# Low parts of the mixers' projection weights: an accumulating DMA in place of a subtraction on GpSimd or VectorE

## The chip, the cores and the metric

One NeuronCore of a Trainium2 chip runs one transformer layer. The metric is device time in microseconds (us) of one execution; the kernel before took 799.82 us, the median of three runs (797.5 to 801.35). Engine names in the views: PE is TensorE's matmul, PEld its weight load, DVE is VectorE, ACT is ScalarE, POOL is GpSimd, SP is the engine that issues most loads.

## The reference, cut to what matters

512 tokens of 1024 features go through one decoder layer. Only its first half is touched by the change:

```python
u = rms_norm(x, g_mix) @ w_in              # 3072 columns: q, k, v of two mixers
ya = diff_attention(qa, ka, va, lam, ...)  # 4 heads, softmax of two score maps
yb = stick_breaking_attention(qs, ks, vs)  # 8 heads, sigmoids and a running product
h = x + concat(ya, yb) @ w_out
h = h + cross_attention(...)               # then the MLP and a last norm
```

All of it is float32. The kernel keeps that precision with three float32r products for each product of matrices.

## The kernel before, in words

**Two parts of a float32.** Each matrix is held as hi + lo, both float32r. `split` (L107) makes them: ScalarE copies the source into hi with rounding (L109), then one engine subtracts, lo = source - hi (L113). `mm3` (L101) issues three products: lines L102, L103 and L104 are hi by hi, hi by lo, lo by hi, in the order of left and right operand. In a projection whose weights are on the right, as for the values (v), it is L103 that reads the weights' lo.

**Pieces of weights.** Weights come in pieces of 128 partitions by 1024 numbers, 512 KB, in the order of the list `stream`. A piece is loaded by SP into a tile `raw` (L122), and `parts` (L125) splits it into tiles `hi` and `lo`. There are three buffers each of raw, hi and lo, so the load of piece n+3 waits until lo of piece n has been made, and hi of piece n+3 waits until TensorE has done with piece n. `take` (L138) hands out a piece and has the next one or two made. The list `lo_eng` says who does the subtraction: VectorE at first, GpSimd from the start of the mixers (L717) up to unit 4, VectorE again from there (L731).

**The mixers.** Units u = 0 to 3 are heads of differential attention, u = 4 to 7 pairs of stick-breaking heads. A unit has four steps (query blocks). In a step TensorE makes scores `sc` (L378 to L382), ScalarE exponentials (L394) or sigmoids (L404, L405), VectorE the weights `e` (L391 to L399, or L407 and L409), and TensorE transposes them (L422) one half-step later. Between the steps `fill` runs projection work of later units on TensorE: how much is in the table `FILL`, which the change leaves alone. The scores have one buffer, so the scores of a step wait until ScalarE has read those of the step before. The projections of the fill are, in this order: keys k1, values va0 (two pieces, a and b), keys k2, k3, values va1 (a, b), then q4, k4, vb0 (a, b), q5, k5, q6, k6, q7, k7, vb1 (a, b); w_out follows (its first piece is called o0 here). Queries and keys of the first mixer go through `rope` (L290), in which VectorE multiplies, GpSimd multiplies (`sh`, L295) and VectorE adds (`rt`, L296); ScalarE and VectorE then write the two parts of q or k.

**What sets the order.** TensorE's order is that of the code. In the mixers ScalarE, VectorE and GpSimd are put in order by the scheduler when the kernel is built; each engine then runs its list strictly in that order.

Of the kernel before, what the change touches and what calls it, by code (L numbers as in the profile page):

```python
# [14 lines left out]
AF = mybir.ActivationFunctionType  # L15
ALU = mybir.AluOpType
# [6 lines left out]
NEG = -1e30  # L23
# pairs of feature tiles of a quarter in the order in which the up projection makes them
DOWN = (0, 2, 1, 3)
EPS = 1e-6
# PE microseconds of filler work after each half of a step, per unit
FILL = (
# [10 lines left out]
TWO_PI = 6.2831853071795864769252867665590057683943  # L39
# ROPE_THETA ** (-arange(0, 16, 2) / 16) in float32  # L40
FREQ = [1.0, 0.1939227432012558, 0.03760603070259094, 0.007292664609849453,
# [4 lines left out]
def two_pi_parts(bits, n):  # L46
    """2 pi as a sum of n floats of the given number of bits each."""
    from decimal import Decimal, getcontext

    getcontext().prec = 60  # L50
    rest = Decimal("6.28318530717958647692528676655900576839433879875021164194988918")
    parts = []
    for _ in range(n):
        e = math.frexp(float(rest))[1]
        unit = Decimal(2) ** (e - bits)
        q = (rest / unit).to_integral_value(rounding="ROUND_DOWN") * unit
        parts.append(float(q))
        rest -= q
    return parts
# [3 lines left out]
def tile_decoder_layer(  # L63
# [34 lines left out]

    # Every matrix product is the sum of three products of parts: a float32 is the
    # exact sum of two float32r, a = hi + lo, and lo * lo lies below float32's last place.  # L100
    def mm3(o, l, r, first, last):  # L101
# [4 lines left out]
    def split(hi, lo, src, scale=1.0, eng=None):  # L106
        """hi + lo = src * scale; scale is a number or a column of one per partition."""  # L107
        if isinstance(scale, float):
            nc.scalar.activation(hi, src, AF.Copy, bias=0.0, scale=scale)  # L109
        else:  # L110
            nc.scalar.activation(hi, src, AF.Identity, bias=0.0, scale=scale)
        if isinstance(scale, float) and scale == 1.0:
            (eng or nc.vector).tensor_tensor(lo, src, hi.bitcast(F32), ALU.subtract)  # L113
        else:
            nc.vector.scalar_tensor_tensor(lo, src, scale, hi.bitcast(F32), ALU.mult, ALU.subtract)

    # Pieces of weights in the order of their use; each is loaded and split some pieces ahead.
    stream, loaded, taken, lo_eng = [], [], [0], [nc.vector]
# [6 lines left out]
    def parts(raw, dst=None):  # L125
        if dst is None:
            dst = [wp.tile(raw.shape, F32R, tag=n, name=n) for n in ("hi", "lo")]
        split(dst[0], dst[1], raw, eng=lo_eng[0])
        return dst
# [13 lines left out]
    def proj_n(act, o, n, last=8, ahead=2):  # L143
        """o = (act @ w)^T for the next 128 columns of weights and an activation with features
        first; what the steps cost on TensorE."""
        whi, wlo = take(ahead)
# [10 lines left out]
    def rsqrt(pool, v, n, name, eng=None):  # L157
        """v ** -0.5 for a few columns: a guess from the exponent and three Newton steps."""
        y = pool.tile([P, n], F32, tag=name, name=name)
# [74 lines left out]

# [1 line left out]
    ident = cp.tile([P, P], F32, name="ident")  # L236
# [8 lines left out]
    for i in range(2):  # L245
        m = cp.tile([P, P], BF16, name=f"mask{i}")
        nc.gpsimd.memset(m, 0.0)
        # kept where q - k - i >= 0
        nc.gpsimd.affine_select(m, m, pattern=[[-1, P]], compare_op=ALU.is_ge, fill=NEG,
# [7 lines left out]
    R = cp.tile([P, 8, S], F32, name="resid")  # L257
# [1 line left out]
    att = ExitStack()  # L259
# [7 lines left out]

    # A query tile holds two heads of 64 features: q[h] has the two parts of head h below each other,
    # hi in its own rows; k[h] has hi of head h in both halves, k[2] lo of both heads in their rows.
    def q_tiles():  # L270
# [70 lines left out]

    # Work that fills TensorE between the steps of the mixers, in its order.
    class Filler:
# [20 lines left out]
    class Mixer:  # L364
        """One step of a mixer: a head of differential attention, or a pair of stick-breaking heads."""

# [4 lines left out]
        def scores(self, i):  # L371
            """Scores of query block i against the keys up to its end, for both halves of the rows."""
            q, k = self.qk
# [37 lines left out]
        def transpose(self, i):  # L411
            """Weights of query block i into blocks i, i + 3, ... (one for each key block)."""
            if not self.w:
# [66 lines left out]
    def by_key(w, j):  # L480
        """Weights of key block j, and the columns of query tokens they go to."""
        b0 = 11 if j == 3 else 4 * j
# [61 lines left out]

    # x with features first waits in DRAM for the residual
    x_ps = {}
# [25 lines left out]

    # TensorE runs at its full clock only after some microseconds of work
    wps = mm_tile()
# [41 lines left out]
    fill = Filler()  # L616
    # angles, and their remainders by 2 pi in three steps, each exact
    freq = sp.tile([P, 8], F32, name="freq")
# [15 lines left out]
    nc.gpsimd.tensor_scalar(ang, ang, math.pi - 2e-7, -(math.pi - 2e-7), ALU.min, ALU.max)  # L634
    # cos(a) = sin(pi / 2 - |a|)
    anc = sp.tile([P, 4, 8], F32, name="anc")
# [7 lines left out]
    nc.scalar.activation(cs, anc, AF.Sin, bias=0.0, scale=1.0)  # L644
    # the queries and keys of the first mixer are an eighth; put_k makes the keys whole again
    rsx = rs8.unsqueeze(2)
# [26 lines left out]
    put_k(ks[0], rope(ps), 8.0)  # L673
    # lambda
    lp = sp.tile([P, 2, 64], F32, name="lp")
# [12 lines left out]

# [1 line left out]
    def add_qk(u):  # L690
# [25 lines left out]
    add_v(vb, 1, vb_tile, vb_proj)  # L716
    lo_eng[0] = nc.gpsimd  # L717
    fill.run(9.1)

    prev = None  # L720
    for u in range(8):
# [7 lines left out]
        fill.unit = u  # L729
        if u == 4:  # L730
            lo_eng[0] = nc.vector  # L731
# [32 lines left out]

# [1 line left out]
    bp = ctx.enter_context(tc.tile_pool(name="bp", bufs=1, reuse_waits="tile"))  # L766
# [58 lines left out]

# [1 line left out]
    kx = [xp.tile([P, 8, M], F32R, name=f"kx{i}") for i in range(2)]  # L827
    vx = [xp.tile([P, 2, D], F32R, name=f"vx{i}") for i in range(2)]
    for n in range(8):
# [3 lines left out]
        if n == 1:  # L833
            # scale of the queries, folded into the softmax
            tr = tr_tile().rearrange("p (t n) -> p t n", t=4)
# [109 lines left out]

# [1 line left out]
    # The up projection is done in 2 x 2 blocks (of features, of inputs, of tokens) with Winograd's seven  # L947
    # products for eight: for W = A11 .. A22 (feature block, input block) and activations B11 .. B22
    # (input block, token block)
    #   S1 = A21 + A22, S2 = S1 - A11, S3 = A11 - A21, S4 = A12 - S2  # L950
    #   T1 = B12 - B11, T2 = B22 - T1, T3 = B22 - B12, T4 = T2 - B21
    #   U2 = A11 B11 + S2 T2, U3 = U2 + S3 T3
    #   C11 = A11 B11 + A12 B21, C12 = U2 + S1 T1 + S4 B22, C21 = U3 - A22 T4, C22 = U3 + S1 T1
    ml = ctx.enter_context(tc.tile_pool(name="ml", bufs=1, reuse_waits="tile"))
# [52 lines left out]
    def weave(a, b):  # L1007
        """Steps of two lists in turn."""
        return [x for pair in itertools.zip_longest(a, b) for x in pair if x is not None]

    # the steps of the MLP: products of the up projection beside pieces of the down projection
    def up_steps(u):
# [141 lines left out]
    def up_norm():  # L1154
        for t in range(4):
            junk = wp.tile([P, D], F32, tag="raw", name="junkh")
            nc.scalar.activation(junk, acc[:, t, :], AF.Square, bias=0.0, scale=1.0, accum_out=ss[:, t:t + 1])
        # relu(r u)^2 = r^2 relu(u)^2 for r > 0: the square of the scale goes onto the down products
        nc.gpsimd.tensor_scalar(ss, ss, 1.0 / D, EPS, ALU.mult, ALU.add)
# [23 lines left out]
    upper_half = slice(512, D)  # L1183
    # the sum of squares of a token and acc * g_final over the columns done
    fs = ml.tile([P, 4, 3], F32, name="fs")
# [13 lines left out]
    for t in range(4):  # L1199
        squares_of(t, 0, slice(0, 512))  # L1200
        gained(t, slice(0, 512))
    # h = -0.5 (mean + eps), the part of it that is done
    nc.vector.tensor_scalar(fc, fs[:, :, 0], -0.5 / D, -0.5 * EPS, ALU.mult, ALU.add)
# [17 lines left out]
    def root(h):  # L1221
        # (-2 h) ** -0.5: a guess from the exponent and three Newton steps
        r = ml.tile([P, 1], F32, tag="fr", bufs=2, name="fr")
# [8 lines left out]
    def finish(t, cols, r):  # L1232
        """cols: the columns that are still to be multiplied by g_final."""
        tok = slice(t * P, (t + 1) * P)
# [54 lines left out]
```

## Time and profile before

| | |
|---|---|
| median of 3 runs | 799.82 us (797.5 to 801.35) |
| span of the profiled execution | 795.6 us |
| PE busy | 769.2 us, 97% of the span |
| DVE, ACT, POOL busy | 553.1, 423.9, 104.7 us |
| the mixers with what is left of the q and k of unit 0 | about 40 to 250 us of the span |

The span runs from the first to the last instruction of one profiled execution, and the median of the timed runs lies 4.2 us above it; the profiled execution has no time of its own beside its span. TensorE is busy nearly all the time, so what can be won or lost is in the few stretches in which it stands still, and in the stretches in which its clock is granted at half.

### The profile page before, as it was taken

Reading aid. Unit: us, or ns where it says so; the run is one execution under the profiler, and the core shown is the slowest. Engines: PE = TensorE matmul, PEld = TensorE weight load, DVE = VectorE, ACT = ScalarE, POOL = GpSimd, SP = SyncE. Lnnn points to the kernel's source line nnn. Section 1 sums busy time; section 2 is a strip of 40 time slices with the busy share of each in tenths; the row PEclk is TensorE's granted clock in tenths of the full one; section 3 lists DMA queues with packets and bytes.
Section 4 is the critical chain, followed back from the end, with each engine's and each line's share of the span. In section 5 each row is a group of like instructions: output and inputs, shape, how many; then the busy total and the mean of one; then the engine's idle time right before and its main releaser. Section 6 shows DMA issues by size and latency. Waiting matters only on the chain.

```text
span 795.6 us, 11669 instructions
## 1 busy us (share of the span) xinstructions
PE 769.2 (97%) x4552; PEld 668.1 (84%) x4552; DVE 553.1 (70%) x829; ACT 423.9 (53%) x723; POOL 104.7 (13%) x200
## 2 busy tenths in 40 slices
PE   7997999999979999999999999999999999999996
PEld 6886788877867899888888899888988899889885
DVE  3889877689896874445746989556865486647745
ACT  5646655777756554254535788333543454345622
POOL 7166443420050011000000030000000000000000
PEclk9998999999989999999999999999999999999998
DMA  9522111211113446224361044332334233230402
GB/s 267 164 81 79 54 54 54 75 35 56 50 53 118 148 130 188 82 77 133 102 191 53 27 162 131 106 107 79 114 99 127 86 92 121 80 105 1 133 1 106
DMA packets 83977, 77.98 MB, mean 98 GB/s; under 512 B 2545, under 2 KB 70290, under 8 KB 83922
## 3 DMA queue, kind: packets, MB, share of 16 engines
q1 hardware_dynamic: 83120, 76.16, 30.8%
q0 software_dynamic: 160, 0.13, 0.4%
q8 instruction: 36, 0.59, 0.3%
q10 hardware_dynamic: 642, 0.93, 0.3%
q14 instruction: 19, 0.16, 0.1%
HBM read 73.03 MB, written 4.19 MB: 97 GB/s over the span
## 4 chain that ended last, share of the span: by engine, by line
PE 84%; DVE 9%; ACT 3%; DMA 1%; issue 1%; POOL 0%; SPq 0%; DVEq 0%; ACTq 0%
PE mm L102 14%; PE mm L103 13%; PE mm L104 13%; PE av L102 5%; PE av L103 5%; PE av L104 5%; PE sc L102 4%; PE sc L103 4%; PE sc L104 4%; PE tr L102 4%; PE tr L104 4%; PE tr L103 4%; PE tr L422 1%; DMA raw<-in_w_in_dram 1%; PE av L451 1%
## 5 line engine op out<-in xcount | busy, mean ns | idle before, releaser
L109 ACT ACTIVATE hi<-raw 128x1024 fp32r<-128x1024 f32 x92 | 97.3, 1057 | 77.7 <-PE tr L103 15.2
L113 DVE TENSOR_TENSOR lo<-raw,hi 128x1024 fp32r<-128x1024 f32 x80 | 99.6, 1245 | 44.7 <-ACT hi L109 43.4
L109 ACT ACTIVATE hi<-blk 128x1024 fp32r<-128x1024 f32 x40 | 42.4, 1061 | 70.1 <-PE sc L104 48.3
L102 PE MATMUL mm<-a,hi 128*128 128x512 f32 x160 | 66.6, 416 | 0.2
L113 DVE TENSOR_TENSOR lo<-blk,hi 128x1024 fp32r<-128x1024 f32 x40 | 48.7, 1221 | 25.9 <-ACT hi L109 25.9
L103 PE MATMUL mm<-a,hi 128*128 128x512 f32 x160 | 63.3, 395 | 0.0
L104 PE MATMUL mm<-a,lo 128*128 128x512 f32 x160 | 63.2, 395 | 0.0
L102 PE MATMUL mm<-b,hi 128*128 128x512 f32 x128 | 50.2, 393 | 0.0
L104 PE MATMUL mm<-b,lo 128*128 128x512 f32 x128 | 50.0, 390 | 0.0
L103 PE MATMUL mm<-b,hi 128*128 128x512 f32 x128 | 49.8, 389 | 0.0
L102 PE MATMUL av<-a,hi 128*128 128x256 f32 (+1 forms) x144 | 42.7, 296 | 0.0
L103 PE MATMUL av<-a,hi 128*128 128x256 f32 (+1 forms) x144 | 42.7, 296 | 0.0
L104 PE MATMUL av<-a,lo 128*128 128x256 f32 (+1 forms) x144 | 42.6, 296 | 0.0
L102 PEld LDWEIGHTS mm<-a,hi 128*128 128x128 f32 x160 | 30.1, 188 | 8.7 <-issue 1.6
L102 PE MATMUL tr<-a,hi 128*128 128x256 f32 x128 | 36.2, 283 | 0.0
L104 PE MATMUL tr<-a,lo 128*128 128x256 f32 x128 | 36.2, 283 | 0.0
L103 PE MATMUL tr<-a,hi 128*128 128x256 f32 x128 | 36.2, 283 | 0.0
L104 PEld LDWEIGHTS mm<-a,lo 128*128 128x128 f32 x160 | 30.1, 188 | 6.9
L103 PEld LDWEIGHTS mm<-a,hi 128*128 128x128 f32 x160 | 30.2, 189 | 5.9 <-POOL a L726 0.2
L102 PE MATMUL mm<-hi,a 128*128 128x256 f32 x112 | 34.4, 307 | 0.0
L103 PE MATMUL mm<-lo,a 128*128 128x256 f32 x112 | 32.6, 291 | 0.0
L104 PE MATMUL mm<-hi,a 128*128 128x256 f32 x112 | 32.5, 291 | 0.0
(388 smaller groups left out, 2346.5 us busy)
## 6 DMA issues: line engine op xcount, KB each, us to landing
blk<-in_w_up_dram SPq DMA_DIRECT2D x32, 512.0 KB, 3.7
raw<-in_w_down_dram SPq DMA_DIRECT2D x32, 512.0 KB, 3.3
raw<-in_w_in_dram SPq DMA_DIRECT2D x24, 512.0 KB, 3.8
raw<-in_w_xkv_dram SPq DMA_DIRECT2D x16, 512.0 KB, 3.9
raw<-in_w_out_dram SPq DMA_DIRECT2D x8, 512.0 KB, 4.0
raw<-in_w_xq_dram SPq DMA_DIRECT2D x8, 512.0 KB, 4.0
raw<-in_w_xo_dram SPq DMA_DIRECT2D x8, 512.0 KB, 4.1
x<-in_x_dram SPq DMA_DIRECT2D x4, 512.0 KB, 8.4
```

The costliest lines, as they stand in the source:

```text
L102: nc.tensor.matmul(o, l[0], r[0], start=first, stop=False)
L103: nc.tensor.matmul(o, l[0], r[1], start=False, stop=False)
L104: nc.tensor.matmul(o, l[1], r[0], start=False, stop=last)
L109: nc.scalar.activation(hi, src, AF.Copy, bias=0.0, scale=scale)
L113: (eng or nc.vector).tensor_tensor(lo, src, hi.bitcast(F32), ALU.subtract)
L422: nc.tensor.transpose(tr[:, j, :], self.es[i][:, h, j * P:(j + 1) * P], ident)
L451: nc.tensor.matmul(o[:, cols], vj, w, start=(j == 0 and part == 0), stop=(j == 3 and part == 1))
```

## The change

For the pieces that are split from the start of the mixers up to unit 7 (before: GpSimd up to unit 4, then VectorE), `parts` now writes -hi into the lo tile by a second copy on ScalarE, with scale -1, and GpSimd issues a DMA that adds raw onto it in place. The DMA's source is the raw tile and its target the lo tile, both in SBUF. The diff also drops comments, which is left out here; line numbers after are up to 7 higher.

```diff
     def parts(raw, dst=None):
         if dst is None:
             dst = [wp.tile(raw.shape, F32R, tag=n, name=n) for n in ("hi", "lo")]
+        if lo_eng[0] == "dma":
+
+            nc.scalar.activation(dst[0], raw, AF.Copy, bias=0.0, scale=1.0)
+            nc.scalar.activation(dst[1], raw, AF.Copy, bias=0.0, scale=-1.0)
+            flat = [a.rearrange("p a b -> p (a b)") for a in (dst[1], raw)]
+            nc.gpsimd.dma_start(flat[0], flat[1], accum_op=ALU.add)
+            return dst
         split(dst[0], dst[1], raw, eng=lo_eng[0])
         return dst
...
-    lo_eng[0] = nc.gpsimd
+    lo_eng[0] = "dma"
     fill.run(9.1)
...
-        if u == 4:
+        if u == 7:
             lo_eng[0] = nc.vector
```

18 pieces are made this way (va0b to vb1b, and o0): 12 that GpSimd subtracted and 6 that VectorE subtracted. TensorE's and SP's lists stay as they were, apart from what their instructions wait for. The lists of ScalarE, VectorE and GpSimd change in their order too.

ScalarE at the first scores of unit 0, before. `k0_594`, `k1_595` are the parts of key k1, `e_691` the first exponentials, `hi_643` the high part of piece k2:

```order
L109 ACTIVATE hi_643<-raw_641 128x1024
L109 ACTIVATE k0_594<-rt_630 64x512
L109 ACTIVATE k1_595<-rt_630 64x512
L286 ACTIVATE k0_594<-rt_630 64x512
L286 ACTIVATE k1_595<-rt_630 64x512
L394 ACT_TABLE_LOAD
L394 ACTIVATE e_691,es_694<-sc_684,nmax_692 128x128 x2
```

The same place now; `lo_645` is written with -hi, and `q0_136`, `q1_137` are the parts of the queries of unit 2:

```order
L130 ACTIVATE hi_644<-raw_642 128x1024
L131 ACTIVATE lo_645<-raw_642 128x1024
L109 ACTIVATE k0_594<-rt_631 64x512
L109 ACTIVATE k1_595<-rt_631 64x512
L293 ACTIVATE k0_594<-rt_631 64x512
L293 ACTIVATE k1_595<-rt_631 64x512
L109 ACTIVATE q0_136<-rt_757 64x512
L109 ACTIVATE q1_137<-rt_757 64x512
L401 ACT_TABLE_LOAD
L401 ACTIVATE e_693,es_696<-sc_686,nmax_694 128x128 x2
```

The negated copy has come in, and the two copies of q have moved ahead of the table load and the first exponentials.

GpSimd at the same place, before. `sh` are the products of `rope`, `lo_601` is the low part of va0b and `lo_644` that of k2:

```order
L295 TENSOR_TENSOR sh_567<-sh_567,sinb_102 128x512
L113 TENSOR_TENSOR lo_601<-raw_598,hi_600 128x1024
L295 TENSOR_TENSOR sh_628<-sh_628,sinb_102 128x512
L113 TENSOR_TENSOR lo_644<-raw_641,hi_643 128x1024
L295 TENSOR_TENSOR sh_753<-sh_753,sinb_102 128x512
```

And now:

```order
L302 TENSOR_TENSOR sh_567<-sh_567,sinb_102 128x512
L133 DMA lo_601<-raw_598 128x1024
L302 TENSOR_TENSOR sh_629<-sh_629,sinb_102 128x512
L302 TENSOR_TENSOR sh_755<-sh_755,sinb_102 128x512
L133 DMA lo_645<-raw_642 128x1024
```

Both subtractions have become DMA issues, and the second stands one product later.

ScalarE in unit 1, before. `sq_1026` are the squares that TensorE sums in the norm of unit 0, `k0_929` to `k1_930` the parts of key k3:

```order
L109 ACTIVATE hi_985<-raw_983 128x1024
L394 ACTIVATE e_1000,es_1003<-sc_993,nmax_1001 128x256 x2
L442 ACTIVATE sq_1026<-av_1013 128x512
L109 ACTIVATE wt0_1028<-tr_1032 128x128
L109 ACTIVATE wt0_1028<-tr_1080 128x2x128
L394 ACTIVATE e_1046,es_1049<-sc_1039,nmax_1047 128x384 x2
L109 ACTIVATE k0_929<-rt_972 64x512
L109 ACTIVATE k1_930<-rt_972 64x512
```

And now:

```order
L130 ACTIVATE hi_990<-raw_988 128x1024
L131 ACTIVATE lo_991<-raw_988 128x1024
L401 ACTIVATE e_1006,es_1009<-sc_999,nmax_1007 128x256 x2
L109 ACTIVATE k0_933<-rt_977 64x512
L109 ACTIVATE k1_934<-rt_977 64x512
L293 ACTIVATE k0_933<-rt_977 64x512
L293 ACTIVATE k1_934<-rt_977 64x512
L449 ACTIVATE sq_1032<-av_1019 128x512
L109 ACTIVATE wt0_1034<-tr_1038 128x128
L401 ACTIVATE e_1052,es_1055<-sc_1045,nmax_1053 128x384 x2
```

The four copies of key k3 have moved from behind the exponentials of the third step to ahead of the squares.

## Rows read from the trace of the kernel before

**Rows 1.** Busy time by stretch; columns: us, five engines, TensorE's granted clock, DMA, GB/s.
```profile
core 0: us, PE busy (x) PEld busy (x) DVE busy (x) ACT busy (x) POOL busy (x), PEclk, DMA share, GB/s
...
59.20:63.60 4.40, 0.07 (x1) 0.00 (x0) 4.26 (x6) 4.31 (x9) 2.64 (x2) 1.00 0.38 119
63.60:70.40 6.80, 6.59 (x30) 6.07 (x31) 6.51 (x11) 5.12 (x13) 5.40 (x4) 0.50 0.00 0
...
87.20:150.00 62.80, 62.69 (x429) 54.35 (x430) 47.15 (x100) 38.67 (x91) 27.37 (x53) 1.00 0.17 50
150.00:218.00 68.00, 67.09 (x391) 54.60 (x390) 58.62 (x99) 50.87 (x105) 8.10 (x24) 1.00 0.21 63
...
227.50:238.00 10.50, 5.27 (x22) 4.92 (x22) 9.45 (x13) 3.23 (x6) 2.08 (x5) 0.67 0.27 80
```

**Rows 2.** PE in order of time: start, length, instruction, idle before.
```profile
51.93 0.28 PE L103 MATMUL tr<-lo,a 128*128 128x256 f32 x1
...
63.81 0.80 PE L378 MATMUL sc<-k,q 128*128 128x256 f32 x2 [4.55 <-DVE rt L296]
...
87.14 0.66 PE L422 MATMUL tr<-ident,e 128*128 128x128 f32 x4 [1.06 <-DVE e L399]
```

**Rows 3.** GpSimd's subtractions in order of time.
```profile
48.41 2.85 POOL L113 TENSOR_TENSOR lo<-raw,hi 128x1024 fp32r<-128x1024 f32 x1
...
56.10 2.39 POOL L113 TENSOR_TENSOR lo<-raw,hi 128x1024 fp32r<-128x1024 f32 x1
```

**Rows 4.** VectorE in order of time, from the same stretch.
```profile
43.80 0.69 DVE L296 TENSOR_TENSOR rt<-rt,sh 128x512 f32<-128x512 f32 x1 [1.19 <-POOL sh L295]
...
49.05 2.77 DVE L296 TENSOR_TENSOR rt<-rt,sh 128x512 f32<-128x512 f32 x1
...
56.58 2.45 DVE L296 TENSOR_TENSOR rt<-rt,sh 128x512 f32<-128x512 f32 x1
...
83.16 2.66 DVE L398 TENSOR_SCALAR e<-e,es 128x512 f32<-128x512 f32 x1
```

**Rows 5.** ScalarE in order of time, up to the first exponentials.
```profile
45.83 1.06 ACT L109 ACTIVATE hi<-raw 128x1024 fp32r<-128x1024 f32 x1
...
59.07 1.28 ACT L109 ACTIVATE k<-rt 64x512 fp32r<-64x512 f32 x2 [3.53 <-DVE rt L296]
...
61.66 1.28 ACT L394 ACT_TABLE_LOAD   x1
```

**Rows 6.** DMA issues: output and input, engine, count, KB each, median us to landing.
```profile
raw<-in_w_in_dram SPq DMA_DIRECT2D x24, 512.0 KB, 3.8
...
out_dram<-resid SPq DMA_DIRECT2D x3, 256.0 KB, 2.4
...
lv<-in_lambda_q_dram POOLq DMA_DIRECT2D x2, 32.0 KB, 7.5
```

**Rows 7.** ScalarE in unit 1, in order of time.
```profile
93.07 0.59 ACT L442 ACTIVATE sq<-av 128x512 f32<-128x512 f32 x1
```

**Rows 8.** PE in unit 1, in order of time.
```profile
94.27 1.05 PE L463 MATMUL av<-ones,sq 128*128 128x2 f32 x8
```

**Rows 9.** ScalarE at the first step of unit 3, in order of time.
```profile
127.47 1.06 ACT L109 ACTIVATE hi<-raw 128x1024 fp32r<-128x1024 f32 x1 [1.85 <-issue]
...
131.19 0.37 ACT L394 ACTIVATE e<-sc,nmax 128x128 f32<-128x128 f32 x1
...
131.89 0.59 ACT L109 ACTIVATE wt<-tr 128x512 fp32r<-128x512 f32 x1
```

**Rows 10.** PE in units 2 and 3, in order of time.
```profile
130.33 0.28 PE L103 MATMUL mm<-lo,a 128*128 128x256 f32 x1
...
132.37 0.40 PE L378 MATMUL sc<-k,q 128*128 128x256 f32 x2
```

**Rows 11.** ScalarE at the piece vb0b, in order of time.
```profile
121.12 1.06 ACT L109 ACTIVATE hi<-raw 128x1024 fp32r<-128x1024 f32 x1 [2.32 <-POOL rso_t L170]
122.09 0.57 ACT L109 ACTIVATE q<-mm 64x512 fp32r<-64x512 f32 x1
```

## What the change is predicted to do

> **What bounds the kernel now.** I read the busy time by stretch first, then TensorE's idle moments in its timeline, then the engines that end them. TensorE is the bound: from 87.2 to 150 us it is busy for 62.69 of 62.80 us, and from 150 to 218 for 67.09 of 68.00 [rows 1]. There a faster VectorE or GpSimd can bring at most 0.11 and 0.91 us. What can be won lies in a few places. From 59.2 to 63.6 TensorE works for 0.07 us; the scores at 63.81 come after 4.55 us of idle, and from 63.6 to 70.4 the clock is granted at 0.50, the lower of its two levels, 1.2 of 2.4 GHz [rows 1, 2]. At 87.14 another 1.06 us of idle end with an e of VectorE [rows 2]. The last hole, about 227.5 to 238 (5.27 of 10.50 us busy, clock 0.67) [rows 1], is in unit 7, whose pieces go by VectorE before and after the change; I leave it as it is.
>
> What fills the hole at 59 is a chain over three engines. VectorE's addition `rt` takes 0.69 us when GpSimd is quiet, but 2.77 at 49.05 and 2.45 at 56.58 [rows 4]. These two overlap GpSimd's subtractions, which start at 48.41 and 56.10 and last 2.85 and 2.39 [rows 3]: both end 0.55 us after the subtraction does (51.82 after 51.26, 59.03 after 58.49), about their own length. So a subtraction on GpSimd holds up VectorE operations that read two SBUF operands. Behind the second one ScalarE writes k (from 59.07, two pairs of 1.28), loads a table at 61.66 for 1.28, and makes the exponentials [rows 5], which free the scores' buffer for 63.81.
>
> **What goes.** 12 subtractions leave GpSimd (2.39 each) and 6 leave VectorE. On the chain to 63.81 the two blocked additions give back 2.77 - 0.69 = 2.08 and 2.45 - 0.69 = 1.76, together 3.84 us [rows 4]. The e operation at 83.16, 2.66 long, is of the same kind [rows 4], and so the idle 1.06 before 87.14 [rows 2] should go. In the stretches where TensorE is full the relief has nothing to shorten.
>
> **What comes on ScalarE.** Each of the 18 pieces costs one more copy of the size of hi, 1.06 us [rows 5], 19.1 us in all, and the list of ScalarE changes. Four places matter.
> 1. Before the first exponentials now stand two copies of q. They have the size of the k pair, 1.28 us [rows 5]. The scores then start at 63.81 - 3.84 + 1.28 = 61.25, a gain of 2.56.
> 2. Between the exponentials of the second and third step of unit 0 stand two pairs hi and -hi, not two hi: 2 x 1.06 = 2.12 us more. If the clock stays at its upper level behind the shorter hole, TensorE's 6.59 us of work in the slow stretch [rows 1] take half of that, a gain of 3.3; of it 3.3 - 2.12 = 1.2 stays, for the third step's exponentials then end the wait. One copy of wt that now stands before the fourth step's exponentials (0.5 to 0.9, by the copies of its size near 0.59 [rows 9]) takes another 0.9. With the 1.06 at 87.14 the balance at 87 us is 2.56 + 1.2 - 0.9 + 1.06 = 3.9 us gained.
> 3. In unit 1 the squares started at 93.07 [rows 7], right behind the exponentials; now four copies of k (2 x 1.28) come first, so the squares run from 95.63 to 96.22. TensorE wants them at 94.27 [rows 8] and its list is unchanged: 1.95 us lost.
> 4. In unit 3 hi of piece q5 starts at 127.47 and the first exponentials at 131.19 [rows 9]. Between them now also stand -hi, 1.06, and the wt of 0.59 that followed them [rows 9]. The two exponentials (0.37 each) end at 131.19 + 1.65 + 0.74 = 133.58; the scores at 132.37 [rows 10] wait for them: 1.2 us lost.
> Elsewhere ScalarE has 50.87 of 68 us busy from 150 to 218, and about 6 more copies there make 57.2 [rows 1]; I cost these at nothing, since TensorE's own work covers them. If that cover failed at each of the six, it would be up to 6.4 us.
>
> **What comes on GpSimd and the DMA queues.** No row shows an accumulating DMA. It reads 512 KB of raw and 512 KB of the low part and writes 512 KB, all in SBUF. Bounds from rows: a plain load of 512 KB lands 3.8 us after issue, a store of 256 KB after 2.4 [rows 6], so 256 KB cost about 1.4 and a second read of 512 KB might add 2.8: 6.6 in all. The low end is 2.4, if SBUF is quicker than HBM; the high end is the 7.5 of GpSimd's own small DMAs [rows 6], which ran beside the first loads. I take 5.2, the middle of 3.8 and 6.6, nearest to the row of the same size. The first piece, va0b, is the tight one: its subtraction ended at 51.26 [rows 3] and TensorE reads it at 51.93 [rows 2]. Now hi and -hi end at 45.83 + 2.12 = 47.95 [rows 5], GpSimd issues where the subtraction stood, at 48.41, and the data land at 53.6. TensorE stands still for 1.7 us at 51.93. This is hidden: without it TensorE would be idle again from 59.26 (63.81 - 4.55) to 61.25, 2.0 us. The stall costs nothing until the landing takes 5.5 us, and each us above that costs one. The next tight piece is vb0b: -hi ends at 122.66 + 1.06 = 123.72 (behind the hi and q of 121.12 and 122.09 [rows 11]), landing at 128.9, and TensorE reads it at 130.33 [rows 10]: free until the landing takes 6.6. The following loads wait for the DMA where they waited for GpSimd; they have many us of room.
>
> A row on the other side: the e at 83.16 is a TENSOR_SCALAR on float32 in SBUF, and was 2.66 long beside GpSimd [rows 4], so the two engines hold each other up. The Trainium skill, SBUF — State Buffer, section "SBUF: two separate sides", says that this goes for DMA issues too: while VectorE runs an operation that takes both ports, GpSimd can't write the descriptors, and its DMA waits. Up to 63.81 VectorE mostly runs operations of two tensors, for which that page expects no such stop. No row here shows a DMA issue of GpSimd beside a busy VectorE. By the rule a few issues would come one VectorE operation late, under 1 us, and only at va0b would it count: the sum would be up to 0.7 us worse.
>
> **The sum.** 3.9 - 1.95 - 1.2 = 0.7 us gained, against the execution of 795.6: 794.9. The median stands 4.2 above that span, so 799.8 - 0.7 = 799.1 us.
>
> **Rivals.**
> - Faster, because the relief counts and the new places on ScalarE don't: the squares and the exponentials of unit 3 find slack that their timeline doesn't show, or TensorE comes there later than I think. Then 2.56 + 3.3 + 1.06 = 6.9 us are gained: 792.9 us. For it: the blocked additions are plain in the rows. Against it: the list of ScalarE, which is strict. Chance 0.25.
> - Slower, because the accumulating DMA is slow. The deciding point is the landing time: 5.5 us for va0b, 6.6 for vb0b. At 10 us va0b lands at 58.4, TensorE stands still for 6.5 and reaches the scores at 65.8, 2.0 later than before; vb0b lands at 133.7 and costs 3.4; the places 3 and 4 stay at 3.15, one more key piece may cost 1.8, and the 1.06 is gained: 2.0 + 3.4 + 3.15 + 1.8 - 1.06 = 9.3 us, 809.1 us. For it: three streams of 512 KB and the 7.5 of rows 6. Against it: DMA share in these stretches is 0.38 at most [rows 1]. Chance 0.22.
> - The change doesn't relieve VectorE: making the descriptors on GpSimd blocks it as the subtraction did. Then 3.84 aren't won, the q pair costs 1.28, places 3 and 4 cost 3.15: about 4.4 slower, 804.2 us. For it: GpSimd still has work at the same places. Against it: the data of a DMA don't pass through GpSimd, so an issue should hold it for less time than a subtraction of 2.39 us. Chance 0.10.
>
> **How the numbers follow.** My forecast has 0.43, the rivals 0.25, 0.22 and 0.10. A difference under 0.5% (4 us) can't be told from none here, so faster means under 795.8 and slower over 803.8. The forecast lies within, the first rival below, the two others above: faster 0.25, same 0.43, slower 0.32. The range takes in the first rival and most of the second: 792 to 809. The forecast's own range, with landings of 3.8 to 7.5, is 797 to 803.
>
> **What would show it.** Right: `rt` at about 49 and 56 lasts 0.7; the idle before the second scores is under 1 us and the clock stays up behind it; a stop of 1 to 2 us at L103 of the first values; a wait of about 2 us of TensorE for the squares of unit 1, and about 1 us in unit 3; accumulating DMAs landing in 4 to 6.5 us. Wrong: landings over 7 us, TensorE waiting for lo at more than one piece, additions that stay at 2.5 us, or no wait at the squares.

## The result and the profile after

The changed kernel takes 793.64 us (median of 10 runs, 791.15 to 796.39) against 797.56 for the kernel before in the same series (10 runs): a ratio of 0.9943, 95% interval 0.9922 to 0.9965, or 3.9 us gained. That lies inside the predicted range, but 5.5 us below the point and its 0.57% is just past the bound of 0.5%, which the interval still takes in: by the measured ratio the change is faster, where I had forecast no difference that can be told. The profiled execution spans 791.5 us, 4.1 less than the 795.6 of before.

By stretch (columns as in [rows 1]):
```profile
59.20:63.60 4.40, 3.21 (x25) 2.73 (x25) 3.65 (x9) 4.32 (x10) 3.86 (x3) 1.00 0.46 134
63.60:70.40 6.80, 6.80 (x48) 5.96 (x47) 5.29 (x10) 5.84 (x12) 3.88 (x4) 1.00 0.26 51
...
87.20:150.00 62.80, 60.85 (x415) 52.57 (x415) 39.23 (x92) 41.29 (x94) 15.31 (x52) 1.00 0.46 100
150.00:218.00 68.00, 67.39 (x407) 55.46 (x406) 54.84 (x96) 57.94 (x112) 13.87 (x32) 1.00 0.47 110
```
TensorE now works 3.21 us between 59.2 and 63.6 where it worked 0.07, and the granted clock from 63.6 to 70.4 is 1.00 (2.4 GHz), not 0.50. From 87.2 to 150 it has lost something: 60.85 us busy, before 62.69.

TensorE's waits in order of time (start, length, instruction, idle before and what ended it):
```profile
53.68 0.36 PE L103 MATMUL tr<-lo,a 128*128 128x256 f32 x1 [1.39 <-ACT hi L130]
...
62.28 0.39 PE L385 MATMUL sc<-k,q 128*128 128x256 f32 x1 [1.19 <-ACT e L401]
...
71.97 0.50 PE L385 MATMUL sc<-k,q 128*128 128x512 f32 x1 [0.87 <-ACT e L401]
...
77.09 0.38 PE L385 MATMUL sc<-k,q 128*128 128x256 f32 x1 [0.52 <-ACT e L401]
...
82.25 0.60 PE L429 MATMUL tr<-ident,e 128*128 128x128 f32 x4
...
90.31 0.94 PE L470 MATMUL av<-ones,sq 128*128 128x2 f32 x7 [1.22 <-ACT sq L449]
...
129.05 0.51 PE L385 MATMUL sc<-k,q 128*128 128x256 f32 x2 [0.74 <-ACT e L401]
```
Against [rows 2, 8, 10] the scores stand at 62.28 (63.81 before), the transposes at 82.25 (87.14), the sums of squares at 90.31 (94.27), the scores of unit 3 at 129.05 (132.37). The first wait is put down to ScalarE's hi, which was done by 47.1; what came last was the landing of the low part, at 53.54. So TensorE is 4.9 us ahead at 82, loses a microsecond at 90 and again at 129 in waits that before did not have, is 3.2 ahead at 140, and ends 4.1 ahead.

The 3.2 us come from two things. From 40 to 140 us TensorE's idle times of 0.45 us and more sum to 6.73 before and 5.93 after, 0.8 less. And the half clock is gone: the matmuls from the first scores to the one below took 70.36 - 63.81 = 6.55 us before and take 65.99 - 62.28 = 3.71 now, 2.8 less (first line before, second after).
```profile
70.36 0.31 PE L104 MATMUL mm<-hi,a 128*128 128x256 f32 x1
```
```profile
65.99 0.28 PE L104 MATMUL mm<-hi,a 128*128 128x256 f32 x1
```
Together that is 3.6 us; counted at the matmuls the lead grows by 3.4, from 0.2 behind at 41 us, ahead of every change, to 3.2 ahead at 140. Most of what is left to 4.1 comes between 165 and 220 us, where the lead grows from 3.2 to 3.9 in small steps. In the largest step the transposes no longer wait for VectorE's part of `wt` (before, then after):
```profile
176.01 0.79 PE L422 MATMUL tr<-ident,e 128*128 128x128 f32 x5 [0.64 <-DVE wt L113]
```
```profile
172.14 0.33 PE L429 MATMUL tr<-ident,e 128*128 128x128 f32 x1
```

GpSimd, VectorE and ScalarE at the places of [rows 3 to 5, 7], one fence for each:
```profile
48.61 0.96 POOL L133 DMA_DIRECT2D lo<-raw  x1
52.96 2.67 POOL L302 TENSOR_TENSOR sh<-sh,sinb 128x512 f32<-128x512 f32 x2 [3.39 <-DVE sh L299]
55.58 0.89 POOL L133 DMA_DIRECT2D lo<-raw  x1
```
```profile
49.24 0.69 DVE L303 TENSOR_TENSOR rt<-rt,sh 128x512 f32<-128x512 f32 x1
...
54.68 1.50 DVE L303 TENSOR_TENSOR rt<-rt,sh 128x512 f32<-128x512 f32 x1
...
67.07 0.48 DVE L406 SCALAR_TENSOR_TENSOR e<-e,es 128x256 f32<-128x256 f32 x1
```
```profile
58.82 1.28 ACT L109 ACTIVATE q<-rt 64x512 fp32r<-64x512 f32 x2
60.12 1.28 ACT L401 ACT_TABLE_LOAD   x1
...
87.20 1.28 ACT L109 ACTIVATE k<-rt 64x512 fp32r<-64x512 f32 x2
88.50 1.27 ACT L293 ACTIVATE k<-rt 64x512 fp32r<-64x512 f32 x2
89.68 0.57 ACT L449 ACTIVATE sq<-av 128x512 f32<-128x512 f32 x1
```
The additions `rt` that took 2.77 and 2.45 us take 0.69 and 1.50. The second still overlaps GpSimd's rope products (52.96 to 55.63), which also read two operands from SBUF. The squares stand behind four k copies, as foreseen. And one row that I had not used: before, VectorE's `e` and TensorE's wait for it were (VectorE, then TensorE)
```profile
70.89 2.52 DVE L399 SCALAR_TENSOR_TENSOR e<-e,es 128x256 f32<-128x256 f32 x1
```
```profile
73.47 0.44 PE L422 MATMUL tr<-ident,e 128*128 128x128 f32 x2 [1.12 <-DVE e L399]
```
It ran beside the next pair of subtractions on GpSimd; now it takes 0.48 (at 67.07), and the wait of 1.12 us is gone.

The new transfers on the page of the profile (output and input, queue, count, KB each, median us to landing), and their issues by source line (ns shortest/median/longest):
```profile
lo<-raw POOLq DMA_DIRECT2D x18, 512.0 KB, 4.7
```
```profile
L133 POOL DMA_DIRECT2D lo<-raw x18: 847/858/962, 48.6 to 201.6; - x18
```

### The profile page after: what moved, and what is told of

Read it like the earlier page. It is cut to its first block, busy times and chain, and to the rows that moved or that the text cites. A ratio compares the mean times of both kernels' runs of the same rounds, so it can differ in the third digit from the quotient of the medians.

```text
span 791.5 us, 11716 instructions
## 1 busy us (share of the span) xinstructions
PE 765.8 (97%) x4552; PEld 665.2 (84%) x4552; DVE 535.0 (68%) x823; ACT 439.1 (55%) x741; POOL 90.0 (11%) x206
## 4 chain that ended last, share of the span: by engine, by line
PE 87%; ACT 5%; DVE 4%; issue 1%; DMA 1%; POOL 0%; SPq 0%; DVEq 0%; ACTq 0%
PE mm L102 14%; PE mm L103 14%; PE mm L104 14%; PE av L102 5%; PE av L103 5%; PE av L104 5%; PE sc L102 4%; PE sc L104 4%; PE sc L103 4%; PE tr L104 4%; PE tr L102 4%; PE tr L103 4%; PE av L458 2%; PE tr L429 1%; DMA raw<-in_w_in_dram 1%
## 5 line engine op out<-in xcount | busy, mean ns | idle before, releaser
L113 DVE TENSOR_TENSOR lo<-raw,hi 128x1024 fp32r<-128x1024 f32 x74 | 92.3, 1248 | 43.9 <-ACT hi L109 42.8
L109 ACT ACTIVATE hi<-raw 128x1024 fp32r<-128x1024 f32 x74 | 78.2, 1057 | 70.9 <-PE tr L103 15.2
L102 PE MATMUL mm<-hi,a 128*128 128x256 f32 x112 | 33.2, 297 | 0.0
L109 ACT ACTIVATE hi<-s 128x1024 fp32r<-128x1024 f32 x16 | 17.0, 1062 | 27.4 <-PE sc L104 14.6
L104 PE MATMUL mm<-hi,a 128*128 128x256 f32 x112 | 31.6, 282 | 0.0
```

The source lines that it names most:

```text
L102: nc.tensor.matmul(o, l[0], r[0], start=first, stop=False)
L104: nc.tensor.matmul(o, l[1], r[0], start=False, stop=last)
```

## The experiments

e7, e11 and e12 add work whose result nothing reads, e8 and e9 a copy that is overwritten; the others only hand the same work to other engines. Ratios are to the kernel before in the same series, whose medians were 797.2, 797.5 and 797.1.

| | kernel | median us | ratio, 95% interval |
|---|---|---|---|
| e1 | DMA for the first 12 pieces, VectorE for the last 6 | 793.0 | 0.9943 (0.9923 to 0.9963) |
| e2 | GpSimd for the first 12, DMA for the last 6 | 796.9 | 0.9993 (0.9971 to 1.0015) |
| e3 | before, DMA for the first 2 pieces only | 791.1 | 0.9910 (0.9880 to 0.9940) |
| e4 | VectorE for all pieces | 793.3 | 0.9933 (0.9907 to 0.9959) |
| e5 | after, squares given priority | 793.8 | 0.9946 (0.9926 to 0.9966) |
| e6 | after, first piece on VectorE | 795.5 | 0.9965 (0.9944 to 0.9986) |
| e7 | before, matmuls put into the hole | 796.9 | 0.9983 (0.9964 to 1.0003) |
| e8 | after, negated copy made twice | 803.8 | 1.0077 (1.0052 to 1.0102) |
| e9 | e3 and negated copies in the other 16 | 801.6 | 1.0052 (1.0034 to 1.0070) |
| e10 | e3 and DMA for the fifth piece | 790.0 | 0.9901 (0.9880 to 0.9922) |
| e11 | after, a plain DMA ahead of each accumulation | 806.7 | 1.0118 (1.0096 to 1.0140) |
| e12 | after, two subtractions back on GpSimd | 798.0 | 1.0018 (1.0002 to 1.0033) |

**e1 and e2: which pieces bring the gain.**
```diff
 # e1, against after
-        if u == 7:
+        if u == 4:
             lo_eng[0] = nc.vector
 # e2, against after
-    lo_eng[0] = "dma"
+    lo_eng[0] = nc.gpsimd
...
+        if u == 4:
+            lo_eng[0] = "dma"
         if u == 7:
             lo_eng[0] = nc.vector
```


> The accumulating DMA makes the low parts of the twelve pieces that GpSimd made before; VectorE keeps the last six (units 4 to 6). Theory A (the gain is made before 87 us, where GpSimd's subtractions no longer block VectorE's): the time is that of the changed kernel, 793.6 us, within 1.5 us, and against before it is 0.3 to 0.7% faster. Theory B (relief of VectorE by six subtractions of 0.6 to 2.5 us counts): 2 us or more slower than the changed kernel, 796 us or above.

> GpSimd makes the low parts of the first twelve pieces as before, the accumulating DMA only those of the last six, which VectorE made. Theory A: the time of before, 797.6 us, within 1.5 us, since TensorE's gain all stood by 87 us. Theory B: it keeps 1.5 us or more of the gain, 796 us or below.


e1 is as fast as the change, e2 as slow as before. Theory A holds in both: what the medians can tell comes from the pieces that GpSimd had. The traces show that the relief of VectorE in units 4 to 6 is small, not nothing. From 165 to 220 us TensorE gains 0.65 to 0.76 us on the trace of before in the five kernels in which the DMA makes the last six pieces and nothing is added at them (the change, e2, e5, e6, e12). In the four in which VectorE makes them (e1, e3, e4, e10) it loses 0.02 to 0.08.

e2 also shows that the cost of GpSimd's subtractions differs from one execution to the next. Its profiled execution was a long one (800.4 us, the median is 796.9). There two operations `e` in a row were held up, for 2.53 and 2.44 us, and the transposes that wait 1.12 us in the trace of before waited
```profile
74.28 0.69 PE L429 MATMUL tr<-ident,e 128*128 128x128 f32 x2 [4.62 <-DVE e L406]
```

**e3: the first two pieces alone.**
```diff
+        if lo_eng[0] is nc.gpsimd and made[0] < 2:
+            made[0] += 1
+            nc.scalar.activation(dst[0], raw, AF.Copy, bias=0.0, scale=1.0)
+            nc.scalar.activation(dst[1], raw, AF.Copy, bias=0.0, scale=-1.0)
...
+            nc.gpsimd.dma_start(flat[0], flat[1], accum_op=ALU.add)
+            return dst
```


> The kernel before, with the accumulating DMA for the first two pieces alone (the second half of the first v tile and the third k). Theory A (these two subtractions, at 48.4 and 56.1 us, blocked VectorE's rope products): the first score matmul of the hole at 59 to 64 us starts 1.2 to 1.8 us earlier, and of the 4.9 us that the changed kernel is ahead at its transpose at 82 us 3 to 5 us are there; the time is 793 to 795.5 us. Theory B (each later subtraction on GpSimd blocks as much): less than half of the gain, 796 us or above.


791.1 us: more than the whole gain, and 2 us better than A's band. TensorE's waits up to 80 us:
```profile
51.69 0.36 PE L103 MATMUL tr<-lo,a 128*128 128x256 f32 x1 [1.76 <-DMA lo<-raw]
...
59.88 0.39 PE L385 MATMUL sc<-k,q 128*128 128x256 f32 x1 [0.75 <-ACT e L401]
...
73.63 0.50 PE L385 MATMUL sc<-k,q 128*128 128x256 f32 x2 [0.58 <-ACT e L401]
79.77 0.44 PE L429 MATMUL tr<-ident,e 128*128 128x128 f32 x2 [0.82 <-DVE e L406]
```
They sum to 3.91 us, and no wait of 0.45 us follows up to 140 us, while the change has 1.22 and 0.74 more at 90 and 129 us. No half clock comes between 40 and 140 us either. By waits and clock that is 6.73 - 3.91 + 2.84 = 5.7 us against the trace of before. Matmul by matmul, the lead grows by 5.2 us from 41 to 140 us, where the changed kernel's grows by 3.4. The two executions can't be compared by their starts alone: at 41 us, ahead of every change, e3's is already 2.2 us ahead (the granted clock up to there averages 1.00, before 0.96). Of the 3.93 us by which the scores at 59.88 come earlier, 1.8 are then due to the two pieces, and of the lead at the transposes 5.2: the upper end of A's first band, and just past its second.

So the other ten pieces that GpSimd had cost more on the DMA than they bring: the waits of 1.22 + 0.74 = 1.96 us are what the change gives back. By the times alone this isn't shown, since the intervals of e3 and of the change overlap (up to 0.9940, from 0.9922); it rests on the traces.

**e4: VectorE for all.**
```diff
-    lo_eng[0] = nc.gpsimd
+    lo_eng[0] = nc.vector
```


> The kernel before with VectorE making all low parts: no GpSimd subtraction, no accumulating DMA. Theory A (what GpSimd's subtraction cost was VectorE's operations beside it): twelve subtractions of about 0.7 to 1.3 us on VectorE replace 2.0 to 2.1 us of blocking twice or more each, the hole at 59 to 64 us shrinks by 0.5 to 1.5 us, and the time is 1 to 4 us below before, 794 to 796.5 us. Theory B (the gain is that VectorE has nothing of the split to do): no gain or a loss, 797.5 us or above.


793.3 us, no different from the change, and a little better than A's band. The first critical subtraction on VectorE, and the addition behind it:
```profile
46.97 1.23 DVE L113 TENSOR_TENSOR lo<-raw,hi 128x1024 fp32r<-128x1024 f32 x1
48.11 0.68 DVE L296 TENSOR_TENSOR rt<-rt,sh 128x512 f32<-128x512 f32 x1
```
1.23 us of its own instead of 2.08 more on the addition beside it. The gain is not the DMA's doing; it is GpSimd's not subtracting. It is made up differently, though: TensorE still waits 2.62 us for the scores at 59.80, the clock still falls to half there, for 6.8 us from 59.7, and the gain lies in the waits, 3.86 us from 40 to 140 against 6.73 before.

**e5 and e6: two single waits.**
```diff
 # e5, against after
+                with tc.high_priority(offset=100):
+                    nc.scalar.activation(self.sq, o, AF.Square, bias=0.0, scale=1.0)
 # e6, against after
+        if lo_eng[0] == "dma" and not made:
+            made.append(1)
+            split(dst[0], dst[1], raw, eng=nc.vector)
+            return dst
```


> The changed kernel with the squares of a mixer's output queued earlier on ScalarE, ahead of copies of other pieces. Theory A (TensorE's wait of 1.22 us for the first squares, 89.09 to 90.31 us, is the k copies that stand ahead of them, and what it loses there it never gets back): that wait falls to 0.5 us or less and the time by 0.5 to 1.2 us, to about 792.8 us. Theory B (the wait is taken up by later waits, or the squares displace something as urgent): 793.6 us within 0.5 us, or more.

> The changed kernel with the first of the eighteen pieces made by VectorE, so that no accumulation is waited for at 52 us (TensorE's idle time there was 1.39 us). Theory A (the same time is waited again for the first exponentials at 61 us): the idle time at 52 us goes, that at 61 us grows by about as much, and the time is 793.6 us within 0.7 us. Theory B (the landing's delay is lost for good): 792.3 us or below.


e5 decides nothing: the squares kept their place behind the k copies, TensorE waited 1.22 us as before, and the time is that of the change a second time. That moving the squares would give back the wait stays untested. In e6 the stop at 52 us is gone, and the scores wait instead:
```profile
61.27 0.80 PE L389 MATMUL sc<-k,q 128*128 128x256 f32 x2 [3.94 <-ACT e L405]
```
1.39 + 1.19 us of waits became 3.94 in one, followed by 6.8 us at half clock. B's gain did not come, as A said; but the time is 1.8 us above the change, past A's 0.7. The edit puts a VectorE subtraction of 1.23 us into the chain to the scores, so it does not test the stop alone.

**e7: the clock alone.**
```diff
+            if u == 0 and n == 0:
+                idle = tr_tile()
+                for _ in range(60):
+                    nc.tensor.matmul(idle[:, :P], identb, identb, start=True, stop=True)
```


> The kernel before with sixty matmuls of 128 columns whose results nothing reads, put into the first half step, so that TensorE works in the hole at 59 to 64 us. Theory A (the clock at half from 63.6 to 70.4 us was a part of the gain, 3.3 us by the prediction, and its sum took ScalarE's copies from it): the clock stays at 1.00 from 62 to 70 us, TensorE is early at the scores there, and the transpose at 73.5 us, which waits for VectorE's blocked product, gives 2 to 3 us back of it at most; the time is 794.5 to 796.5 us. Theory B (what is late there is VectorE and ScalarE, the clock hides behind them): 797.6 us within 0.7 us, or slower by the time of the added matmuls (60 of some 55 to 110 ns).


796.9 us, theory B: against before -0.17% (-0.36 to +0.03). The clock stayed at 1.00 from 62 to 70, and TensorE waited at
```profile
63.67 0.50 PE L378 MATMUL sc<-k,q 128*128 128x256 f32 x2 [1.15 <-ACT e L394]
...
69.56 0.33 PE L422 MATMUL tr<-ident,e 128*128 128x128 f32 x1 [1.19 <-DVE va L115]
71.22 0.62 PE L378 MATMUL sc<-k,q 128*128 128x384 f32 x2 [1.32 <-ACT e L394]
```
and 3.4 us at half clock came from 72.7 on, so only a part of the slow stretch went. A faster TensorE alone finds VectorE and ScalarE late: the three waits above sum to 3.7 us. What the clock gives counts only where that chain is shortened with it.

**e8 and e9: ScalarE's copies.**
```diff
 # e8, against after
             nc.scalar.activation(dst[1], raw, AF.Copy, bias=0.0, scale=-1.0)
+            nc.scalar.activation(dst[1], raw, AF.Copy, bias=0.0, scale=-1.0)
 # e9, against e3: in the 16 other pieces, ahead of the split
+            nc.scalar.activation(dst[1], raw, AF.Copy, bias=0.0, scale=-1.0)
```


> The changed kernel with each copy of the negated high part made twice: eighteen more ScalarE copies of about 0.95 us. Theory A (ScalarE's added copies cost TensorE only at the prediction's places 2 to 4, about 0.9, 1 and 0.8 us now): those waits grow by 0.5 to 1 us each and the time by 1.5 to 3 us, to 795 to 796.6 us. Theory B (ScalarE's copies are free): 793.6 us within 0.5 us. Theory C (they cost all their time, 17 us): 805 us or more.

> The kernel with the accumulating DMA for the first two pieces alone (791.1 us), and in the sixteen later pieces a ScalarE copy of the negated high part whose result the subtraction then overwrites: the copies of the changed kernel without its DMAs. Theory A (after 92 us the changed kernel gives back what ScalarE's added copies cost): the lead over before that stood at 87 to 92 us falls by 2 to 3 us by 150 us, as in the changed kernel, and the time is 793 to 794.5 us. Theory B (the waits for landings, not the copies, cost it): 791.1 us within 1 us.


e8 loses 10.1 us to the change, over three times A's upper end; no theory had it. The wait for the squares grew from 1.22 to 1.83, and there are new ones; the four longest between 40 and 220 us are
```profile
53.24 0.36 PE L103 MATMUL tr<-lo,a 128*128 128x256 f32 x1 [1.93 <-DMA lo<-raw]
...
72.58 0.73 PE L386 MATMUL sc<-k,q 128*128 128x512 f32 x2 [1.81 <-ACT e L402]
...
93.62 1.05 PE L471 MATMUL av<-ones,sq 128*128 128x2 f32 x8 [1.83 <-ACT sq L450]
...
159.14 0.48 PE L102 MATMUL mm<-a,hi 128*128 128x512 f32 x1 [1.77 <-DVE vb L115]
```
and the clock fell to half three times between 50 and 100 us, 3.4 us each. One more microsecond of ScalarE at each piece spends the room that hid the first. e9 loses 10.5 us to e3, where A said 2 to 3.4: right in sign and far too small. Its copies also delayed GpSimd's subtraction onto a VectorE addition that e3 had kept clear of (GpSimd, VectorE, TensorE):
```profile
86.06 2.38 POOL L113 TENSOR_TENSOR lo<-raw,hi 128x1024 fp32r<-128x1024 f32 x1
```
```profile
86.13 2.85 DVE L306 TENSOR_TENSOR rt<-rt,sh 128x512 f32<-128x512 f32 x1 [0.25 <-POOL sh L305]
```
```profile
92.12 1.86 PE L473 MATMUL av<-ones,sq 128*128 128x2 f32 x8 [3.96 <-ACT sq L452]
```
The k copies wait for that addition, the squares for them, and the clock falls behind the 3.96 us. So e9 does not price the copies alone.

**e10: the fifth piece too.**
```diff
 # e10, against e3
+        made[0] += lo_eng[0] is nc.gpsimd
-        if lo_eng[0] is nc.gpsimd and made[0] < 2:
-            made[0] += 1
+        if lo_eng[0] is nc.gpsimd and made[0] in (1, 2, 5):
```


> The kernel with the accumulating DMA for the first two pieces alone (791.1 us), and for the fifth piece too (the second half of the second v tile), whose GpSimd subtraction at 75.8 us makes VectorE's product e take 2.67 us there, for which TensorE waits 0.82 us at 79 us. Theory A: that product takes 0.5 us, the wait goes, and the time is 0.5 to 1 us lower, 790.1 to 790.6 us, the lowest of all kernels. Theory B (the added ScalarE copies cost as much): 791.1 us within 0.4 us, or more.


790.0 us, A's number and the lowest median of all; but its interval overlaps e3's, so that it beats e3 isn't shown. Both were measured in other series than the change, with before at 797.1 and 797.2 there and 797.6 here; their medians are 3.6 and 2.6 us under the change's. The product of 2.67 us in e3 takes 0.48 here; in this execution another was caught, beside the pieces still on GpSimd, and TensorE waited 1.65 us for it:
```profile
65.06 2.63 DVE L406 SCALAR_TENSOR_TENSOR e<-e,es 128x256 f32<-128x256 f32 x1
...
77.43 0.48 DVE L405 TENSOR_SCALAR e<-e,es 128x512 f32<-128x512 f32 x1
```

**e11: later landings.**
```diff
+            old = wp.tile([P, 768], F32, tag="old", name="old", bufs=1)
+            nc.gpsimd.dma_start(old, flat[1][:, :768])
             nc.gpsimd.dma_start(flat[0], flat[1], accum_op=ALU.add)
```


> The changed kernel with a plain DMA of 384 KB (raw to a tile that nothing reads) put ahead of each of the eighteen accumulating DMAs on the same queue, so that the accumulation lands later. Theory A (the rival of 809.1 us: landings decide from some 5.5 us on): the low part lands 2 to 4 us later after its issue is asked for, and TensorE's waits for the first and later pieces grow by 1 us or more each at four to eight places: 798 to 805 us. Theory B (the landing has room nearly everywhere but at the first piece): 794 to 796 us.


806.7 us, above A's band, but not by A's mechanism: the landing, counted from its issue, went from 4.7 to only
```profile
lo<-raw POOLq DMA_DIRECT2D x18, 512.0 KB, 5.0
```
What cost most was GpSimd's own queue. The added DMA waits there for the load of raw, and behind it stand the small operations of the norm; GpSimd and then TensorE in unit 2:
```profile
122.81 0.57 POOL L134 DMA_DIRECT2D old<-raw  x1 [7.13 <-DMA raw<-in_w_in_dram]
```
```profile
128.79 0.48 PE L484 MATMUL av<-ident,rb 128*128 128x128 f32 x1 [3.68 <-DVE rb L477]
```
Three such waits for rb take 1.04 + 3.68 + 2.21 = 6.9 us; the wait for the first piece grew from 1.39 to 2.95. The added DMAs also share one buffer, and five of their issues waited for the landing of the one before, 7.0 us in all. What a slow landing by itself would cost was not measured.

**e12: two subtractions back.**
```diff
+            made.append(1)
+            if len(made) < 3:
+                old = wp.tile([P, 768], F32, tag="old", name="old", bufs=1)
+                hi = dst[0].rearrange("p a b -> p (a b)").bitcast(F32)
+                nc.gpsimd.tensor_tensor(old, flat[1][:, :768], hi[:, :768], ALU.subtract)
```


> The changed kernel with a GpSimd subtraction added at each of the first two pieces, on 768 of 1024 columns, into a tile that nothing reads. Theory A (GpSimd's subtraction beside VectorE's rope products is the cost that the change removed): VectorE's product rt takes 2 us or more again at 48 to 58 us, the first scores start 1 to 2 us later than in the changed kernel, and 2.5 to 4.5 us of the time come back: 796 to 798 us. Theory B (the gain came from something else): 793.6 us within 1 us.


798.0 us: all of the gain is gone. GpSimd, VectorE and TensorE:
```profile
49.03 2.30 POOL L138 TENSOR_TENSOR old<-raw,hi 128x768 f32<-128x768 f32 x1
51.28 0.96 POOL L133 DMA_DIRECT2D lo<-raw  x1
```
```profile
49.65 2.23 DVE L308 TENSOR_TENSOR rt<-rt,sh 128x512 f32<-128x512 f32 x1
...
56.62 1.89 DVE L308 TENSOR_TENSOR rt<-rt,sh 128x512 f32<-128x512 f32 x1
```
```profile
56.46 0.55 PE L103 MATMUL tr<-lo,a 128*128 128x256 f32 x1 [3.70 <-DMA lo<-raw]
```
The addition is 2.23 us long again. But the subtraction also holds the DMA's issue until 51.28 (48.61 in the change), and TensorE waits 3.70 us for the landing, so blocking and late issue are mixed; e3 and e4, which have neither, carry the proof.

## Why the prediction was right or wrong

- **The point and the range.** Of the 5.5 us between 799.1 and 793.6, 3.2 are gain that I did not forecast, and 2.3 are the base: three runs of before had a median of 799.82, the ten of the result 797.56. The 4.2 us between median and span compared different executions; wherever a run has both, its time lies 1.7 to 2.3 us above its own span. 793.6 is outside my forecast's own range of 797 to 803. It lies in the stated one because that takes in the first rival, so the range held and the forecast's sum did not.
- **What goes: right, and short by two places.** GpSimd's subtraction held up VectorE, and its going is the gain (e1, e3, e4). I counted the additions before 63.81 and the `e` before 87.14, but not the `e` of 2.52 us at 70.89 and TensorE's wait of 1.12 us for it. And I took the relief of VectorE where TensorE is full for nothing; from 165 to 220 us it brought 0.7.
- **Place 1: right in kind, too large.** 2.56 us forecast, the scores came 1.53 earlier. The second addition fell to 1.50, not 0.69: it ends 0.55 us behind GpSimd's rope product (56.18 after 55.63), as the blocked ones ended behind the subtraction. 0.2 are the later start of this execution.
- **Place 2: this is the step that failed.** I took 2.12 us of ScalarE's copies off the 3.3 us of clock, and 0.9 for wt. The clock did stay up, and gave 2.8; what of the copies reached TensorE there were the waits at 71.97 and 77.09, 0.87 + 0.52 = 1.39 us, where I took 3.0. Together with the missed 1.12 us the lead at the transposes is 4.9 instead of 3.9, in spite of place 1. e7 shows that this is not the clock's doing alone: it comes with the shorter chain.
- **Places 3 and 4: right in kind, too large.** The squares do stand behind the k copies and the exponentials of unit 3 behind -hi; TensorE waits 1.22 and 0.74 us, not 1.95 and 1.2: 1.96 instead of 3.15. The first rival, which counted them at nothing, forecast 792.9 and is the nearer number, but the waits are there; e3, which has none of them, is 1.8 us further ahead at 140 us. Place 3 can cost more than its wait: in the traces of e1 and e6 the clock fell to half for 3.4 us behind that same wait (1.22 and 1.20), which cost e1 another 1.5 us; in those of the change and e5 it did not.
- **The accumulating DMA: right.** 4.7 us to landing against 5.2; va0b landed at 53.54 against 53.6, TensorE stood 1.39 us against 1.7, and e6, which takes that stop away (and puts 1.23 us on VectorE), is no faster. The slow rival's 809 us did not come, and its deciding point was not reached by e11.
- **The descriptors: no block seen, and hardly a test of it.** All 18 issues took 847 to 962 ns, so none waited noticeably while it ran. The addition at 49.24 overlaps the issue at 48.61 and took 0.69 us, which excludes the third rival. The effect that the Trainium skill states (SBUF — State Buffer, "SBUF: two separate sides"), VectorE's two-port operations keeping GpSimd from writing descriptors, did not show in this case. The trace hardly puts it to the test: of VectorE's operations with one input in SBUF only a TENSOR_SCALAR at 78.83 (0.49 us) and a COPY at 164.93 (0.43 us) ran beside an issue (79.23 and 165.19), each for less than 0.2 us.

Step by step the sum missed: +1.1 for the `e` at 70.89, +1.6 at place 2 (3.0 to 1.39), -0.5 for the clock (3.3 to 2.8), +1.2 at places 3 and 4, -1.0 at place 1; 0.7 + 2.4 = 3.1 us, against a lead of 3.2 at 140 us in the two traces. The relief of VectorE between 165 and 220 us adds 0.7. Some 0.3 of the 4.1 us aren't assigned.

## What to carry to other kernels

Look beside every long two-operand operation of GpSimd for VectorE operations that last three times their usual length, and price those, not GpSimd's own time: here two subtractions out of eighteen carried the gain. Move only the pieces that block something on the path; the further ones each paid with a ScalarE copy, and by 140 us the kernel with all of them had gained 3.4 us, the one with two 5.2. A DMA started from GpSimd waits in GpSimd's queue for its data, so what stands behind it waits too.

## What I had not expected of the hardware

- VectorE's subtraction of 128x1024 takes 1.23 us alone, GpSimd's takes 2.39 us and blocks a VectorE operation of 0.5 to 0.7 us to 2.5 to 2.9 us beside it: leaving it on VectorE (e4) is as good as the DMA.
- An accumulation of 512 KB inside SBUF lands after 4.7 us, near a plain load of the same size (3.8 in [rows 6], 4.3 after). Three that were issued 1.9 us behind another one took 5.96 to 6.42, the other fifteen 4.50 to 5.09; eighteen of them raise their queue's share from 0.4% to 6.9%.
- Room on ScalarE runs out abruptly: the first added copy at each piece cost 1.96 us in the two waits behind 87 us, doubling it 10.1 us, in part through the clock.
